# Prompt values in products of 512 columns instead of 256, norm weights spread by TensorE, the first stage's order on three engines written out

## The chip, the cores and the metric

One NeuronCore of one Trainium2 chip runs the whole program. Its engines work side by side, each through its own instructions in order: TensorE (PE, with PEld for its weight loads), VectorE (DVE), ScalarE (ACT), GpSimd (POOL) and SyncE (SP), which issues almost all DMAs of this kernel. The metric is the device time of one execution in microseconds (us); lower is better.

## What is computed

One layer of a hybrid encoder, for two groups with the same weights: a prompt of 1024 rows and a sample of 512 rows, 1024 columns each.

```python
def _rmsnorm(x, g):
    xf = x.astype(jnp.float32)
    y = xf * lax.rsqrt(jnp.mean(xf * xf, axis=-1, keepdims=True) + EPS)
    return (y * g.astype(jnp.float32)).astype(x.dtype)

def _layer(x, norm_g, w_in, ...):
    h = _rmsnorm(x, norm_g)
    proj = jnp.einsum('bld,de->ble', h, w_in)
    (q, f_fw, f_bw, i, z_a, c_B, c_C, c_x, z_b, g_a, g_b) = jnp.split(proj, SPLIT_POINTS, axis=-1)
    o_a = _hgrn2_bidir(q, i, f_fw, f_bw, lb_fw, lb_bw, hnorm_g)
    ...
    return x + jnp.einsum('bld,de->ble', merged, w_o)
```

The change touches only the first stage: the norm h of both groups, and the prompt's part `i` of the projection (the values, 1024 rows by 1024 columns, contraction over 1024).

## The kernel before

A number in float32 is split into a high part (a rounded copy, made by ACT) and a low part (the rest, a subtraction on DVE); `split` at L61 to L64 does that. A product of two split operands is three matmuls (`PASSES`: high by high, high by low, low by high), summed in PSUM.

The first stage works on twelve tiles of 128 rows: tiles 0 to 7 are the prompt, 8 to 11 the sample. For each tile: load (L86), sum of squares on ACT (L92), epsilon on DVE (L93), the power -0.5 on POOL (L81), two multiplications by that and by the norm weights on DVE (L96), eight transposes on PE (L163), and then, for a prompt tile, two splits into the operands `B11`, `B12`, `B21`, `B22` (tiles `s0`, `B12`, `s4`, `s6`), for a sample tile two copies and stores to `hs_d` (L230, L231).

Between the tiles stand the value products. The 1024 columns of weights are taken in four blocks of 256. `value_weights` (L184) loads a block in four pieces of 256 KB, each of two rows of 128, into two buffers `v_raw`, and splits them into buffers `v_h` and `v_l`, seven of each, so that three of the next block's four pieces can be made while the present block is in use. `prompt_values` (L196) makes for each prompt tile 24 matmuls of 256 columns (8 contraction steps by 3 passes, L201), one copy from PSUM to SBUF on ACT (L204) and a store to `v_d` on SP (L205). During the last two blocks DVE and ACT also make the sums `T1` to `T4` of the operands for the next stage (`mixed`, L174), which borrow the two large buffers `w2_raw` of the next stage.

The next stage, `project2` (L281), begins with two loads of 512 KB into `w2_raw` (L286): the first has the blocks a11 and a12, the second a21 and a22. a11 is split for the first product (12 matmuls of 512 columns, L308); four sums on DVE (L290 to L293) are needed before the second. Its pools are opened before the last two blocks of values.

The norm weights are loaded by one DMA that repeats them on all 128 partitions (`gain`, 512 KB, L210). Fourteen matmuls on a tile of zeros (L215) run while nothing is there yet.

In what order the engines and SP's queue take these instructions is set by a scheduler that goes by the program's order and its own estimates; each queue is fixed when the program is built. An instruction at the head of a queue that waits for a semaphore holds all behind it on that queue. Each DMA also uses one of eight semaphores in turn.

## Time and profile before

| | us |
|---|---|
| median of 3 runs (lowest to highest) | 1933.41 (1932.57 to 1936.35) |
| the profiled execution | 1938.16 |
| its span, first to last instruction | 1936.4 |
| PE busy in the span | 1911.7 (99%) |
| DVE busy | 1457.9 (75%) |
| ACT busy | 941.7 (49%) |
| POOL busy | 152.8 (8%) |
| mean granted clock of TensorE, share of full speed | 0.995 |

The profile shows one execution. Busy is the time in which an engine has an instruction under way. The granted clock is 1.0 at 2.4 GHz and 0.5 at 1.2 GHz. "Landing" of a DMA is the time from its issue to the arrival of its last byte. The first value product starts at 11.53 us, the first product of the next stage at 118.56 us, both from the span's start.

### The profile page before, as it was taken

What the parts mean: (1) busy time and instruction counts of PE and PEld (TensorE: products, weight loads), DVE (VectorE), ACT (ScalarE), POOL (GpSimd) and SP (SyncE); (2) the same over time, 40 slices, a digit from 0 to 9 for tenths busy, and PEclk for the clock granted to TensorE, in tenths of its full rate; (3) what the DMA queues carried; (4) which work ended last, traced back from release to release, by engine and by line L of the source; (5) the groups of instructions that cost most, each with busy time, mean ns of one, the idle gap of its engine ahead of it and who ended that gap; (6) DMA issues with size and microseconds to landing.
All of it is one profiled execution on the core that took longest, in us unless ns stands there. A gap on an engine that the chain in (4) does not pass through costs nothing.

```text
span 1936.4 us, 38016 instructions
## 1 busy us (share of the span) xinstructions
PE 1911.7 (99%) x14772; PEld 1612.7 (83%) x14772; DVE 1457.9 (75%) x2423; ACT 941.7 (49%) x1946; POOL 152.8 (8%) x220
## 2 busy tenths in 40 slices
PE   8999999999999999999999999999999999999898
PEld 8988888888888888887888888888888888888786
DVE  7558787878787878786677578777872558898896
ACT  6433434434343444444587567777683333424432
POOL 1000000000000000002122122222220000000000
PEclk8999999999999999999999999999999999999999
DMA  7466666766667676668855555655544966979852
GB/s 214 125 211 231 234 230 234 236 232 231 235 228 238 224 234 237 222 217 319 283 186 196 213 198 181 220 192 187 194 167 168 331 219 196 298 239 308 274 169 76
DMA packets 306436, 427.35 MB, mean 221 GB/s; under 512 B 26192, under 2 KB 178000, under 8 KB 306256
## 3 DMA queue, kind: packets, MB, share of 16 engines
q1 hardware_dynamic: 306256, 424.93, 65.0%
q8 instruction: 116, 1.90, 0.4%
q14 instruction: 64, 0.52, 0.1%
HBM read 254.98 MB, written 169.87 MB: 219 GB/s over the span
## 4 chain that ended last, share of the span: by engine, by line
PE 87%; DMA 5%; DVE 5%; issue 1%; ACT 1%; SPq 0%; POOL 0%; DVEq 0%; POOLq 0%; ACTq 0%
PE pp L308 39%; PE pp L77 21%; PE pw L825 9%; PE pp L201 5%; PE o L537 3%; PE sc L451 3%; PE u L513 2%; PE pp L70 2%; DMA w_raw<-in_w_a 1%; PE u L500 1%; DVE w_l L64 1%; DVE s_l L64 1%; PE sc L485 1%; DMA io<-oz_p 1%; DMA w_l<-wv_d 1%
## 5 line engine op out<-in xcount | busy, mean ns | idle before, releaser
L308 PE MATMUL pp<-s_h,w_h 128*128 128x512 f32 x1120 | 435.9, 389 | 1.2 <-ACT w_h L63 1.2
L308 PE MATMUL pp<-s_l,w_h 128*128 128x512 f32 x1120 | 435.7, 389 | 0.0
L308 PE MATMUL pp<-s_h,w_l 128*128 128x512 f32 x1120 | 435.7, 389 | 0.0
L63 ACT ACTIVATE w_h<-w_raw 128x512 fp32r<-128x512 f32 (+1 forms) x204 | 141.3, 693 | 230.7 <-PE pp L308 151.7
L77 PE MATMUL pp<-s_h,w_h 128*128 128x512 f32 x632 | 250.6, 397 | 2.0 <-ACT K L132 2.0
L308 PEld LDWEIGHTS pp<-s_h,w_h 128*128 128x128 f32 x1120 | 210.2, 188 | 45.4 <-ACT w_h L63 1.9
L308 PEld LDWEIGHTS pp<-s_l,w_h 128*128 128x128 f32 x1120 | 210.2, 188 | 43.6
L308 PEld LDWEIGHTS pp<-s_h,w_l 128*128 128x128 f32 x1120 | 210.2, 188 | 43.6
L77 PE MATMUL pp<-s_h,w_l 128*128 128x512 f32 x632 | 246.4, 390 | 0.0
L77 PE MATMUL pp<-s_l,w_h 128*128 128x512 f32 x632 | 246.2, 390 | 0.0
L313 DVE TENSOR_TENSOR tmp<-pp,tmp 128x512 f32<-128x512 f32 x240 | 165.5, 690 | 106.2 <-PE pp L308 105.0
L63 ACT ACTIVATE w_h<-w_S 128x512 fp32r<-128x512 f32 x160 | 99.4, 628 | 187.9 <-PE pp L308 80.9
L64 DVE TENSOR_TENSOR w_l<-w_raw,w_h 128x512 fp32r<-128x512 f32 (+1 forms) x204 | 155.8, 765 | 37.6 <-ACT w_h L63 37.1
L825 PE MATMUL pw<-s_h,w_h 128*128 128x512 f32 x392 | 153.4, 391 | 2.6 <-ACT w_h L63 2.6
L825 PE MATMUL pw<-s_h,w_l 128*128 128x512 f32 x392 | 153.3, 391 | 2.6 <-DVE w_l L64 2.6
L825 PE MATMUL pw<-s_l,w_h 128*128 128x512 f32 x392 | 153.2, 391 | 0.0
L435 ACT COPY cat<-K 128x512 f32<-128x512 f32 x168 | 111.6, 667 | 65.5 <-DVE K L437 26.9
L77 PEld LDWEIGHTS pp<-s_h,w_h 128*128 128x128 f32 x632 | 118.8, 188 | 25.5 <-ACT K L132 2.4
L77 PEld LDWEIGHTS pp<-s_h,w_l 128*128 128x128 f32 x632 | 118.6, 188 | 25.3
L77 PEld LDWEIGHTS pp<-s_l,w_h 128*128 128x128 f32 x632 | 118.9, 188 | 23.4
L436 ACT COPY cat<-Q 128x512 f32<-128x512 f32 x168 | 112.0, 667 | 29.2 <-DVE Q L438 22.3
L437 DVE TENSOR_TENSOR K<-K,T 128x512 f32<-128x512 f32 x144 | 108.9, 756 | 22.9 <-ACT cat L435 21.0
(187 smaller groups left out, 3301.5 us busy)
## 6 DMA issues: line engine op xcount, KB each, us to landing
w_raw<-in_w_in SPq DMA_DIRECT2D x80, 512.0 KB, 5.3
ws_d<-w_h SPq DMA_DIRECT2D x160, 256.0 KB, 2.5
ws_d<-w_l SPq DMA_DIRECT2D x160, 256.0 KB, 2.5
w_h<-ws_d SPq DMA_DIRECT2D x79, 512.0 KB, 3.7
w_l<-ws_d SPq DMA_DIRECT2D x79, 512.0 KB, 5.3
fkq_d<-sg SPq DMA_DIRECT2D x48, 256.0 KB, 2.3
v_raw<-in_w_in SPq DMA_DIRECT2D x32, 256.0 KB, 3.4
fkq_d<-sk SPq DMA_DIRECT2D x32, 256.0 KB, 2.3
```

Source lines behind the costliest of these rows:

```text
L63: A.activation(hi, src, AF.Copy)
L64: V.tensor_tensor(lo, src, hi.bitcast(F32), op=ALU.subtract)
L77: T.matmul(out, whl[a][:, k, :], rhs(k, b), start=k == 0 and n == 0, stop=k == KT - 1 and n == 2)
L201: T.matmul(pp, B[f"B{k // 4 + 1}{t + 1}"][a][:, k % 4, c * P:(c + 1) * P], parts[k][b], start=k == 0 and m == 0, stop=k == KT - 1 and m == 2)
L308: T.matmul(bank, hl[x][:, k, :], B[b][y][:, k, :], start=k == 0 and i == 0, stop=k == 3 and i == 2)
L313: V.tensor_tensor(out, p, t, op=ALU.add)
L435: A.copy(ap(cat, 0, [[2 * hs, nb], [hs, 2], [1, hs]]), kall)
L436: A.copy(ap(cat, TB, [[2 * hs, nb], [hs, 2], [1, hs]]), qall)
L437: V.tensor_tensor(kall, kall, ap(t, m + 1, [[2, nb], [-m - 1, 2], [0, hs]]), op=ALU.mult)
L451: T.matmul(k.sc[-1][s * Q32:(s + 1) * Q32, li % 4, c, :], kk[:, o:o + Q32], qq[:, t:t + Q32], start=True, stop=True)
L537: T.matmul(p[:, c, :], l, r, start=m == 0, stop=m == len(mms) - 1)
L825: T.matmul(bank, hl[x][:, c:c + P], O[n][y][:, k, :], start=k == 0 and i == 0, stop=k == 3 and i == 2)
```

## The change

- The value weights are taken in two blocks of 512 columns instead of four of 256: 24 matmuls of 512 columns for each tile and block, 384 in all instead of 768, with 16 copies and stores instead of 32, each twice as large. A piece of weights is one row of 128 by 512 columns (256 KB as before), so there are eight pieces in a block.
- The first block's eight pieces are loaded at the very start into the two large buffers `mix` and split by `first_parts`; for three of them the subtraction is on POOL. The second block's go through `value_parts`, two buffers `v_raw`, and `v_h`, `v_l` with nine buffers each.
- `gain` comes from two loads of one partition (2 KB each, issued by ACT, as is that of the identity) and two matmuls of a row of ones by them, copied from PSUM by DVE. There are 6 and 2 warming matmuls in place of 14.
- The order of PE, ACT and DVE in the first stage is written out: tile i + 1 is transposed in the middle of the products of tile i, eight transposes in one piece. What comes after (`mixed`, the last five tiles' products) is written out for PE alone. SP's order is still the scheduler's.
- The pools `rp`, `cs`, `wp` of the next stage are opened after the last value product, not before the last two blocks.

```diff
-WARM = 14
+WARM, WARM_2 = 6, 2
 
...
-        vst, p0st = ExitStack(), ExitStack()
+        vst, p0st, mxst = (ExitStack() for _ in range(3))
         wv, pv = (vst.enter_context(tc.tile_pool(name=n, bufs=1)) for n in ("wv", "pv"))
         psv = vst.enter_context(tc.tile_pool(name="psv", bufs=1, space=PSUM))
+        mx = mxst.enter_context(tc.tile_pool(name="mx", bufs=2, side="right"))
         p0 = p0st.enter_context(tc.tile_pool(name="p0", bufs=2, side="right"))
         B["B12"] = [pv.tile([P, 4, TB], F32R, name=f"B12_{s}") for s in "hl"]
 
...
+        xt, rn = {}, {}
+        def x_load(i):
+            xt[i] = p0.tile([P, D], F32, name="x_sb", bufs=4)
+            load(xt[i], x_tiles[i])
+        def square(i):
+            ss = p0.tile([P, 1], F32, name="ss", bufs=3)
+            A.activation(p0.tile([P, D], F32, name="junk", bufs=1), xt[i], AF.Square, scale=D ** -0.5, accum_out=ss)
+            V.tensor_scalar_add(ss, ss, EPS)
+            rn[i] = rsqrt(p0, ss, "x")
+        def scaled(i):
+            y = xt[i]
+            for c in range(0, D, 512):
+                V.scalar_tensor_tensor(y[:, c:c + 512], y[:, c:c + 512], rn[i], gain[:, c:c + 512],
+                                       op0=ALU.mult, op1=ALU.mult)
+        def transposed(i):
+            for half in range(2):
+                tp = psv.tile([P, 4, P], F32, name="tp", bufs=4)
+                for k in range(4):
+                    T.transpose(tp[:, k, :], xt[i][:, (4 * half + k) * P:(4 * half + k + 1) * P], ident)
+                yield half, tp
+        def tile_parts(i, half, tp):
+            cols = slice(i % CPB * P, (i % CPB + 1) * P)
+            if i < 8:
+                split(*(z[:, :, cols] for z in B[f"B{half + 1}{i // CPB + 1}"]), tp)
+            else:
+                t = p0.tile([P, 4, P], F32, name="hs")
+                A.copy(t, tp)
+                store(hs_d[:, 4 * half:4 * half + 4, cols], t)
 
         def mixed(k):
-            t = wp.tile([P, 4, TB], F32, name="w2_raw", bufs=2)
+            t = mx.tile([P, 4, TB], F32, name="mix")
...
 
...
+        parts = {}
+        def value_rows(col, k):
+            c0 = SPLIT["i"] * P + col
+            return w["w_in"][k * P:(k + 1) * P, c0:c0 + TB]
+        def value_tiles(k):
+            parts[k] = [wv.tile([P, TB], F32R, name=f"v_{s}", bufs=9) for s in "hl"]
+            return parts[k]
+        def value_parts(col, k):
+            raw = wv.tile([P, TB], F32, name="v_raw", bufs=2)
+            load(raw, value_rows(col, k))
+            split(*value_tiles(k), raw)
+        def products(i, pp, ks):
+            for k in ks:
+                for m, (a, b) in enumerate(PASSES):
+                    T.matmul(pp, B[f"B{k // 4 + 1}{i // CPB + 1}"][a][:, k % 4, i % CPB * P:(i % CPB + 1) * P], parts[k][b],
+                             start=k == 0 and m == 0, stop=k == KT - 1 and m == 2)
+        def bank_v():
+            return psv.tile([P, TB], F32, name="pp", bufs=4)
+        def values_out(i, col, pp):
+            s = mx.tile([P, TB], F32, name="st")
+            A.copy(s, pp)
+            store(v_d[i, :, col:col + TB], s)
+        order = ExitStack()
+        order.enter_context(tc.manual_schedule(engines={T.engine, A.engine, V.engine}))
+        x_load(0)
+        gain_row = [mx.tile([P, TB], F32, name="st")[0:1, :] for _ in range(2)]
+        for c, g in enumerate(gain_row):
+            nc.scalar.dma_start(g, w["norm_g"][:, c * TB:(c + 1) * TB])
+        nc.scalar.dma_start(ident, ident_d)
+        raws = [mx.tile([P, 4, TB], F32, name="mix") for _ in range(2)]
+        for k in range(KT):
+            load(raws[k // 4][:, k % 4, :], value_rows(0, k))
+            if k == 1:
+                x_load(1)
+        x_load(2)
+        x_load(3)
+        idle = p0.tile([P, P], F32, name="idle", bufs=1)
+        V.memset(idle, 1.0)
         gain = p0.tile([P, D], F32, name="gain", bufs=1)
-        x_ahead = [x_tile(p0, 0)]
-        load(ident, ident_d)
-        load(gain, w["norm_g"].to_broadcast([P, D]))
-        idle = p0.tile([P, P], F32, name="idle", bufs=1)
-        V.memset(idle, 0.0)
-        for n in range(WARM):
-            T.matmul(psv.tile([P, 4, P], F32, name="tp", bufs=4)[:, 0, :], idle, idle, start=True, stop=True)
-        pure(0)
-        parts = value_weights(0)
-        pure(1)
-        prompt_values(0, parts, 0)
-        for c in range(2, CPB):
-            pure(c)
-            prompt_values(0, parts, c - 1)
-        prompt_values(0, parts, CPB - 1)
-        parts = value_weights(256)
-        for c in range(CPB):
-            y = normed(p0, 8 + c, gain)
-            for half in range(2):
-                t = p0.tile([P, 4, P], F32, name="hs")
-                A.copy(t, transposed(y, half))
-                store(hs_d[:, 4 * half:4 * half + 4, c * P:(c + 1) * P], t)
-            prompt_values(256, parts, c)
+        def warm(n):
+            for _ in range(n):
+                T.matmul(psv.tile([P, 4, P], F32, name="tp", bufs=4)[:, 0, :], idle, idle, start=True, stop=True)
+        warm(WARM)
+        for c, row in enumerate(gain_row):
+            g = psv.tile([P, 4, P], F32, name="tp", bufs=4).rearrange("p a b -> p (a b)")
+            T.matmul(g, idle[0:1, :], row, start=True, stop=True)
+            V.tensor_copy(gain[:, c * TB:(c + 1) * TB], g)
+        warm(WARM_2)
+        def first_parts(k):
+            raw, (hi, lo) = raws[k // 4][:, k % 4, :], value_tiles(k)
+            A.activation(hi, raw, AF.Copy)
+            (G if k in (2, 4, 6) else V).tensor_tensor(lo, raw, hi.bitcast(F32), op=ALU.subtract)
+        square(0)
+        scaled(0)
+        tps = list(transposed(0))
+        first_parts(0)
+        tile_parts(0, *tps[0])
+        first_parts(1)
+        tile_parts(0, *tps[1])
+        first_parts(2)
+        square(1)
+        first_parts(3)
+        scaled(1)
+        first_parts(4)
+        first_parts(5)
+        pp = bank_v()
+        products(0, pp, range(6))
+        tps = list(transposed(1))
+        first_parts(6)
+        first_parts(7)
+        for x in tps:
+            tile_parts(1, *x)
+        square(2)
+        scaled(2)
+        products(0, pp, range(6, 8))
+        values_out(0, 0, pp)
+        def ahead_of(i):
+            if i + 3 < 12:
+                x_load(i + 3)
+            if i + 2 < 12:
+                square(i + 2)
+            yield
+            if i + 1 < 12:
+                for x in list(transposed(i + 1)):
+                    tile_parts(i + 1, *x)
+            if i + 2 < 12:
+                scaled(i + 2)
+            yield
+        for i in range(1, 8):
+            todo = ahead_of(i)
+            next(todo)
+            pp = bank_v()
+            products(i, pp, range(4))
+            next(todo)
+            if i == 7:
+                for k in range(4):
+                    value_parts(TB, k)
+            old = dict(parts)
+            products(i, pp, range(4, 8))
+            values_out(i, 0, pp)
+        for k in range(4, KT):
+            value_parts(TB, k)
+        for i in range(8, 11):
+            todo = ahead_of(i)
+            next(todo)
+            pp = bank_v()
+            products(i - 4, pp, range(4))
+            next(todo)
+            products(i - 4, pp, range(4, 8))
+            values_out(i - 4, TB, pp)
+        order.close()
+        order.enter_context(tc.manual_schedule(engines={T.engine}))
 
...
-        parts = value_weights(512)
         p0st.close()
+        for n, i in enumerate((7, 0, 1, 2, 3)):
+            if n < 4:
+                mixed(n)
+            pp = bank_v()
+            products(i, pp, range(KT))
+            values_out(i, TB, pp)
+        order.close()
+        mxst.close()
+        vst.close()
         rp = outer.enter_context(tc.tile_pool(name="rp", bufs=1, side="right", reuse_waits="tile"))
         cs = right.enter_context(tc.tile_pool(name="cs", bufs=1, side="right", reuse_waits="tile"))
         wp = st.enter_context(tc.tile_pool(name="wpp", bufs=1, side="right", reuse_waits="tile"))
-        for col in (512, 768):
-            if col > 512:
-                parts = value_weights(col)
-            for c in range(CPB):
-                prompt_values(col, parts, c)
-                if c % 2 == 0:
-                    mixed((col - 512) // 128 + c // 2)
-        vst.close()
```

From the first dozen instructions of the next stage on, the order on every engine is the same in both programs. Three places where it differs follow. A number in a name is that of one tile.

SP's queue around the change from one block of weights to the next, before (`v_raw_977` to `v_raw_995` are the four pieces of the third block, `st_586` is the last tile of the first):

```order
L205 DMA v_d_67<-st_502 128x256
L191 DMA v_raw_609<-in_w_in 128x2x256
L191 DMA v_raw_977<-in_w_in 128x2x256
L205 DMA v_d_67<-st_530 128x256
L205 DMA v_d_67<-st_558 128x256
L191 DMA v_raw_983<-in_w_in 128x2x256
L191 DMA v_raw_989<-in_w_in 128x2x256
L205 DMA v_d_67<-st_586 128x256
L231 DMA hs_d_66<-hs_623 128x4x128
L231 DMA hs_d_66<-hs_631 128x4x128
```

The same place now (`v_raw_644` to `v_raw_689` are pieces 2 to 7 of the second and last block, `st_590` and `st_668` are the outputs of tiles 6 and 7 from the first):

```order
L219 DMA v_d_67<-st_590 128x512
L179 DMA hs_d_66<-hs_624 128x4x128
L179 DMA hs_d_66<-hs_627 128x4x128
L204 DMA v_raw_644<-in_w_in 128x512
L204 DMA v_raw_650<-in_w_in 128x512
L219 DMA v_d_67<-st_668 128x512
L204 DMA v_raw_671<-in_w_in 128x512
L204 DMA v_raw_677<-in_w_in 128x512
L204 DMA v_raw_683<-in_w_in 128x512
L204 DMA v_raw_689<-in_w_in 128x512
```

Before, pieces of a later block stand among the stores of an earlier one; now six of the second block's eight stand around and behind the last store of the first block. `v_raw_644` waits for the subtraction of piece 0 and `v_raw_650` for that of piece 1, and so on by twos.

ACT at the same place now (`v_h_634` to `v_h_652` are the high parts of pieces 0 to 3, `pp_601` is the bank of tile 7):

```order
L178 COPY hs_624<-tp_614 128x512
L178 COPY hs_627<-tp_619 128x512
L63 ACTIVATE v_h_634<-v_raw_632 128x512
L63 ACTIVATE v_h_640<-v_raw_638 128x512
L63 ACTIVATE s2_h_92<-mix_883 128x512
L63 ACTIVATE s1_h_90<-mix_883 128x512
L63 ACTIVATE s5_h_98<-mix_883 128x512
L63 ACTIVATE v_h_646<-v_raw_644 128x512
L63 ACTIVATE v_h_652<-v_raw_650 128x512
L218 COPY st_668<-pp_601 128x512
```

and before:

```order
L204 COPY st_558<-pp_533 128x256
L63 ACTIVATE v_h_607<-v_raw_609 128x512
L63 ACTIVATE v_h_975<-v_raw_977 128x512
L204 COPY st_586<-pp_561 128x256
L230 COPY hs_623<-tp_624 128x512
L230 COPY hs_631<-tp_632 128x512
```

Pieces 2 and 3 of the new block now stand ahead of the copy of tile 7's output, which stood behind one piece of a block two further on.

SP's queue at the end of the stage, before (`st_1236` to `st_1389` have six more outputs behind them; `w2_raw_1558` is the first pair of the next stage):

```order
L205 DMA v_d_67<-st_1236 128x256
L286 DMA w2_raw_1558<-in_w_in 128x8x128
L205 DMA v_d_67<-st_1264 128x256
L286 DMA w2_raw_1558<-in_w_in 128x8x128
L205 DMA v_d_67<-st_1316 128x256
L300 DMA ws_d_69<-w2_h_1570 128x512
L205 DMA v_d_67<-st_1344 128x256
```

and now (`st_1088` is the output of the last value product, `w2_raw_1111` the first pair of the next stage):

```order
L219 DMA v_d_67<-st_970 128x512
L219 DMA v_d_67<-st_1015 128x512
L219 DMA v_d_67<-st_1060 128x512
L448 DMA v_raw_1785<-in_w_in 128x512
L219 DMA v_d_67<-st_1088 128x512
L373 DMA w2_raw_1111<-in_w_in 128x8x128 x2
L373 DMA w2_raw_1276<-in_w_in 128x8x128
```

Both loads that the next stage begins with have moved from among the stores to behind the last of them.

## Rows read from the trace of the kernel before

**Rows 1.** The chain that ended last, by engine (page, part 4).

```profile
PE 87%; DMA 5%; DVE 5%; issue 1%; ACT 1%; SPq 0%; POOL 0%; DVEq 0%; POOLq 0%; ACTq 0%
```

**Rows 2.** Stretches: length; busy us (instructions) by engine; granted clock, DMA share, GB/s.

```profile
15.00:19.00 4.00, 3.65 (x17) 3.65 (x18) 2.75 (x7) 3.31 (x7) 1.07 (x2) 0.50 0.76 259
60.00:100.00 40.00, 40.00 (x337) 40.00 (x336) 28.72 (x49) 17.95 (x36) 0.00 (x0) 1.00 0.36 105
118.50:123.00 4.50, 3.30 (x15) 2.42 (x15) 2.49 (x6) 1.87 (x4) 0.00 (x0) 1.00 0.30 87
```

**Rows 3.** PE in order of time: first and last value product from 100 us on.

```profile
100.08 0.28 PE L201 MATMUL pp<-v_h,s_l 128*128 128x256 f32 x1
...
118.44 0.28 PE L201 MATMUL pp<-v_h,s_l 128*128 128x256 f32 x1
```

**Rows 4.** PE in order of time: 512-column products of the next stage, first and last.

```profile
328.91 0.39 PE L308 MATMUL pp<-s_h,w_h 128*128 128x512 f32 x1
...
344.78 0.39 PE L308 MATMUL pp<-s_l,w_h 128*128 128x512 f32 x1
```

**Rows 5.** PE in order of time: transposes among value products (start, us, idle before).

```profile
26.32 0.28 PE L201 MATMUL pp<-v_h,s_l 128*128 128x256 f32 x1
26.44 0.60 PE L163 MATMUL tp<-ident,x_sb 128*128 128x128 f32 x4
26.79 0.36 PE L201 MATMUL pp<-v_h,s_h 128*128 128x256 f32 x1
26.99 0.28 PE L201 MATMUL pp<-v_l,s_h 128*128 128x256 f32 x1
...
33.06 0.63 PE L163 MATMUL tp<-ident,x_sb 128*128 128x128 f32 x4 [0.66 <-issue]
```

**Rows 6.** The start in order of time, PE and DVE.

```profile
1.08 5.51 PE L215 MATMUL tp<-idle 128*128 128x128 f32 x28 [1.08 <-DVE idle L213]
7.80 1.41 DVE L96 SCALAR_TENSOR_TENSOR x_sb<-x_sb,rs_x,gain 128x512 f32<-128x512 f32 x2 [1.90 <-DMA gain<-in_norm_g]
11.53 0.58 PE L201 MATMUL pp<-v_h,s_h 128*128 128x256 f32 x1 [1.09 <-ACT s_h L63]
```

**Rows 7.** Groups by line and shape: xcount, busy us, mean ns, idle before; POOL's over the span.

```profile
L92 ACT ACTIVATE junk<-x_sb 128x1024 f32<-128x1024 f32 x12 | 12.7, 1057 | 11.1 <-DMA x_sb<-in_x_prompt 6.6 <-POOL rs_x L81 3.7 <-DMA x_sb<-in_x_sample 0.9
L63 ACT ACTIVATE v_h<-v_raw 128x512 fp32r<-128x512 f32 x16 | 10.1, 629 | 4.6 <-DMA v_raw<-in_w_in 3.7 <-PE pp L201 0.6
L64 DVE TENSOR_TENSOR v_l<-v_raw,v_h 128x512 fp32r<-128x512 f32 x16 | 10.9, 688 | 21.0 <-ACT v_h L63 21.0
L425 POOL TENSOR_TENSOR T<-F 128x512 f32<-128x512 f32 x24 | 27.6, 1151 | 1006.4 <-DMA F<-fkq_d 849.2 <-DVE Q L438 93.7 <-DVE F L134 63.6
```

**Rows 8.** Landings by tile: `v_raw` (66 to 95 us), then `w2_raw` (90 to 112 us).

```profile
DMA to landing us min/median/max: 2.8/2.9/3.0
...
DMA to landing us min/median/max: 4.1/4.8/5.9
```

**Rows 9.** What SP's queue waited for, first 125 us: total us, times, longest.

```profile
SPq L205 <- ACT st L204: 45.3, 25, 2.8
SPq L191 <- DVE v_l L64: 14.1, 9, 3.5
```

**Rows 10.** The end of the values in order of time: ACT, SP, ACT, PE.

```profile
118.80 0.37 ACT L204 COPY st<-pp 128x256 f32<-128x256 f32 x1 [2.51 <-PE pp L201]
119.61 0.38 SPq L361 DMA_DIRECT2D v_raw<-in_w_in  x1
121.50 0.59 ACT L317 COPY tmp<-pp 128x512 f32<-128x512 f32 x1 [2.33 <-PE pp L308]
122.67 0.50 PE L308 MATMUL pp<-s_h,w_h 128*128 128x512 f32 x1 [1.20 <-ACT w_h L63]
```

**Rows 11.** Late in the program: PE in order of time, then the stretch's granted clock.

```profile
1812.91 0.50 PE L825 MATMUL pw<-s_h,w_h 128*128 128x512 f32 x1 [1.00 <-ACT w_h L63]
1815.26 0.63 PE L825 MATMUL pw<-s_h,w_l 128*128 128x512 f32 x1
1817.39 0.63 PE L825 MATMUL pw<-s_l,w_h 128*128 128x512 f32 x1
...
1815.00:1818.00 3.00, 3.00 (x9) 2.33 (x8) 3.00 (x5) 2.43 (x4) 0.00 (x0) 0.50 0.84 278
```

More of the change, by code (lines that the diff above doesn't have):

```diff
@@ L82, in rsqrt @@
         return r
-    def x_tile(pool, i):
-        y = pool.tile([P, D], F32, name="x_sb", bufs=5)
-        load(y, x_tiles[i])
-        return y
-    def normed(pool, i, gain, ahead=()):
-        y = ahead.pop(0) if ahead else x_tile(pool, i)
-        ss = pool.tile([P, 1], F32, name="ss")
-        A.activation(pool.tile([P, D], F32, name="junk", bufs=1), y, AF.Square, scale=D ** -0.5, accum_out=ss)
-        V.tensor_scalar_add(ss, ss, EPS)
-        r = rsqrt(pool, ss, "x")
-        for c in range(0, D, 512):
-            V.scalar_tensor_tensor(y[:, c:c + 512], y[:, c:c + 512], r, gain[:, c:c + 512], op0=ALU.mult, op1=ALU.mult)
-        return y
     keep = ctx.enter_context(tc.tile_pool(name="keep", bufs=1, reuse_waits="tile"))
@@ L157, in trunk_kernel @@
         B["B12"] = [pv.tile([P, 4, TB], F32R, name=f"B12_{s}") for s in "hl"]
-        def transposed(y, half):
-            tp = psv.tile([P, 4, P], F32, name="tp", bufs=4)
-            for k in range(4):
-                T.transpose(tp[:, k, :], y[:, (4 * half + k) * P:(4 * half + k + 1) * P], ident)
-            return tp
-        def pure(c):
-            for t in range(2):
-                y = normed(p0, t * CPB + c, gain, x_ahead)
-                for half in range(2):
-                    n, cols = f"B{half + 1}{t + 1}", slice(c * P, (c + 1) * P)
-                    tp = transposed(y, half)
-                    split(*(z[:, :, cols] for z in B[n]), tp)
+        xt, rn = {}, {}
@@ L182, in mixed @@
                 split(*(z[:, k, :] for z in B[n]), q[x])
-        def value_weights(col):
-            parts = []
-            for k in range(0, KT, 2):
-                hl = [wv.tile([P, 2, 256], F32R, name=f"v_{s}", bufs=7) for s in "hl"]
-                raw = wv.tile([P, 2, 256], F32, name="v_raw", bufs=2)
-                c0 = SPLIT["i"] * P + col
-                load(raw, w["w_in"][k * P:(k + 2) * P, c0:c0 + 256].rearrange("(k p) c -> p k c", p=P))
-                split(*hl, raw)
-                parts += [[z[:, i, :] for z in hl] for i in range(2)]
-            return parts
@@ L196, in prompt_values @@
-        def prompt_values(col, parts, c):
-            for t in range(2):
-                pp = psv.tile([P, 256], F32, name="pp", bufs=4)
-                for k in range(KT):
-                    for m, (a, b) in enumerate(PASSES):
-                        T.matmul(pp, B[f"B{k // 4 + 1}{t + 1}"][a][:, k % 4, c * P:(c + 1) * P], parts[k][b],
-                                 start=k == 0 and m == 0, stop=k == KT - 1 and m == 2)
-                s = pv.tile([P, 256], F32, name="st", bufs=2)
-                A.copy(s, pp)
-                store(v_d[t * CPB + c, :, col:col + 256], s)
```

1 line of the change is left out of this document (removed).

## The prediction

> **What bounds the kernel now.** First the chain of waits by engine: PE holds 87% of it, DMA and DVE 5% each [rows 1]. So time is won by shortening PE's own work or lost by leaving it idle, and an engine beside it counts only where PE waits for it. Then the same stretch of values by windows: from 60 to 100 us PE is busy 40.00 of 40.00 at clock 1.00, while DVE is at 28.72, ACT at 17.95 and the DMAs at 0.36 [rows 2]. Nothing waits there, although SP's queue waits 25 times for a copy on ACT (45.3 us in all) and nine times for a subtraction of weights (14.1 us) [rows 9]: these waits are covered by loads that stand a block ahead. The two ends are another matter. Between 15 and 19 us PE is busy 3.65 of 4.00 at clock 0.50, and from 118.5 to 123 it works 3.30 of 4.50 [rows 2]. Since the order of every engine is the same from the first dozen instructions of the next stage on, only the first 123 us can change. I count up to the start of the second product of the next stage, 122.67 us [rows 10], and add what changes to the profiled execution's 1938.16 us, which is 4.75 above the median of 1933.41.
>
> **Products, −5.1.** From the first to the last row there are 153 steps in 18.36 us, 0.1200 each [rows 3]; 512 columns take 70 steps in 15.87 us, 0.2267 each [rows 4]. 768 × 0.1200 = 92.2 becomes 384 × 0.2267 = 87.1. All of it lies on PE's path. In cycles at 2.4 GHz the rows are 288 and 544, each 32 over the columns.
>
> The Trainium skill ("TensorE: Matmul & The Clock Gate", section "Back-to-back issue gap") gives a warm gap of N/2.4 + 2.5 ns, which speaks against this change: two small products would cost only 2.5 ns more than one large one. By that the term would be 384 × 2.5 ns = 1.0 us, an estimate from the page, and the sum below +16.1 in place of +12.0. The rows show an excess of 13 ns a product, so here the measurement decides.
>
> **Transposes, −0.5.** A group of four makes the step from 26.44 to its last neighbour longer: 26.32 to 26.99 is 0.67 with two products of 0.12 in it, so 0.43 a group [rows 5]. There are 24 groups, 10.3 us. Twelve groups of eight lose one change of kind each; I take 0.78 a group, with 0.74 to 0.86 as bounds (−1.4 to 0; I use −1.0 to 0, as two buffers must be free at once). **Bubble, −0.7.** Idle 0.66 ahead of the transposes at 33.06, put down to PE's own issue [rows 5], belongs to a place in the old order that is gone; −0.8 to 0.
>
> **Start, −1.8.** Before, 118.56 us (118.44 + 0.12) less 92.2, 10.3 and the bubble of 0.8 leaves 15.3 us that PE lost at the start. The first scaling waits 1.90 us for the repeated load of `gain` and starts at 7.80; the first product starts at 11.53 [rows 6]. Now `gain` comes from 2 KB loads, two products of a row of ones, and two copies. No row has such a product. 512 columns in one pass at the low clock took 0.427 (2.13 / 5) [rows 11]; a warming product of 128 columns takes 5.51 / 14 = 0.39 [rows 6], and four times that is 1.6. So 0.43 to 1.6 each, and a copy like a subtraction, 0.69 [rows 7]. With the square (1.06 us [rows 7]) running beside it, scaling starts between 7.4 and 9.2, and the first product, which no longer has the second half's scaling and other tiles' work ahead of it, at 9.9 to 11.7; I take 10.8. From there 18 products at 0.427 end at 18.5, eight transposes at 19.1, six products at 0.227 at 20.5. By then 24 × 0.227 + 2 × 0.78 = 7.0 us of work is done, so 13.5 is lost. Bounds −3.0 to +1.0 (a POOL subtraction of 512 columns takes 1.15 us [rows 7] and three stand in this chain).
>
> **The second block's weights, +10.3.** Here the wide pieces are made through two `v_raw` buffers, and each raw buffer is free only when its subtraction on DVE is done. The order of SP shows pieces 2 to 7 around and behind the last store of the first block; each pair must go round: load issued, landing 2.9 [rows 8], split 0.63, subtraction 0.69 [rows 7], with 0.1 for the next issue 4.3 us, and 4.4 to 4.6 with the second of a pair. PE consumes a pair of rows in 6 × 0.227 = 1.36. In the old order the same waits existed [rows 9], but the pieces stood a block earlier and the spare buffers held three of four. Now seven spare pieces are missing: eight buffers of nine are still read by the last tile of the first block, which is followed at once by the second block.
>
> Let 0 be the start of tile 6's products (near 52 us). Tiles 6 and 7 are 2 × (5.44 + 0.78) = 12.4, so the second block could start at 12.4 and have its first tile done at 18.7. Piece 0 is ready about then: DVE has the scaling, `mixed` sums and the two subtractions in one queue. Piece 2 loads only then, and on ACT its split stands behind three `mixed` splits, each of which waits for a sum on DVE; seven DVE instructions of about 0.69 stand between the subtractions of piece 1 and piece 2, so that is 17.1, piece 3 at 17.8. The store of tile 7 waits for ACT's copy (0.59 [rows 10]) and holds piece 4 behind it on SP until 17.9; it lands at 20.9 and is ready at 22.4, piece 5 at 23.6, pieces 6 and 7 (loads at 22.5 and 23.7) at 26.9 and 28.2. PE's last three products end at 29.0. 29.0 − 18.7 = 10.3. Bound below 8 (landings of 2.8 and `mixed` work one step earlier), above 12.5 (another 0.7 on each of three round trips). What the store and copy wait for cost nothing before, since the cover was a whole block.
>
> **Clock, +2.5.** Late in the program, after PE had idled 1.00 us, the stretch 1815 to 1818 was at 0.50 with PE busy 3.00 of 3.00 [rows 11]; at the start the clock was still 0.50 at 15 to 19 us, up to 7.5 us after the first product [rows 2, 6]. A PE starved in pieces of 2 to 4 us should fall to the low level and be held there when it is fed again. A low stretch of 3.0 to 7.5 us loses about half; I take 5.2 us, 2.5. Bounds 0 to 3.4.
>
> **Next stage's weights, +7.3.** Before, both loads of `w2_raw` stood among the stores, six outputs ahead of the end, and the first product followed the last value product directly. Now both stand behind the last store, which waits for ACT's copy of the last product. With T as the end of values: copy 0.1 + 0.59, store issue 0.38 [rows 10], so loads go out at T + 1.1; landing 4.4, between the lowest 4.1 and the median 4.8 [rows 8] as little else is in flight; split 0.63; PE at T + 6.3. It has then idled longest of all, so twelve products at 0.427 take 5.1, and the second product starts at T + 11.4; its own operands (0.69 sum, 0.63, 0.69 behind the second load) are there by T + 9. Before this was 122.67 − 118.56 = 4.1. So +7.3; 5.9 with landing 4.1 and the clock rising half way, 8.5 with landing 5.6.
>
> **Sum.** −5.1 − 0.5 − 0.7 − 1.8 + 10.3 + 2.5 + 7.3 = +12.0: profiled 1950.2, median 1945.4. All ends low give +4.0 (1937.4), all high +20.3 (1953.7).
>
> **Rivals.** *Worse on ACT and DVE* (1950, chance 0.14): the written order puts copies for the sample's tiles and `mixed` splits ahead of weight splits, and one late sum holds all. Each of the three round trips grows by 0.9 and a second low stretch of 5 us follows: +2.7 and +2.4, sum +17. For it: DVE already has 28.72 of 40 us [rows 2].
>
> *PE stays fed* (faster; 1925.3, chance 0.06): the second block's pieces keep ahead as they did [rows 9] and the next loads find their cover, so only −5.1 − 0.5 − 0.7 − 1.8 = −8.1 remains. This needs both stalls away; it decides the sign where together they (with the clock) cost less than 8.1 us. Against it, a pair takes over 4.3 us round and PE uses it in 1.36, and the loads of the next stage stand literally behind the last store.
>
> *Only the end stalls* (same; 1932.6, chance 0.07): −8.1 + 7.3 = −0.8, if the early pieces land while tile 7 is still running. *Only the weights stall* (1938.1, slower, chance 0.04): −8.1 + 12.8 = +4.7, if PE's idle time at the end is covered by work of the first products as before.
>
> *Products gain little* (1949.5, chance 0.03): if 0.1200 holds waits that wide products inherit and both forms run at their columns alone, 5.1 becomes 1.0. The rows of both forms are back to back [rows 3, 4], which speaks against it; the page above is the rule behind this one.
>
> **How the numbers follow.** The forecast, both stalls, has 0.66. A time within 0.2% (3.9 us, about what a measurement here can tell) is 1929.5 to 1937.3. Slower: 0.66 + 0.14 + 0.04 + 0.03 = 0.87, less 0.02 for the forecast's lowest edge, 0.85; same 0.07 + 0.02 = 0.09; faster 0.06. The range 1936 to 1952 takes in the forecast's bounds but for its highest edge, and three rivals; it leaves out the two rivals that lack the weights' stall.
>
> **What would show it.** *Products:* starts 0.227 apart in the first block; 0.24 would be wrong. *Start:* first product at 10.8, tile 1's at 20.5, no wait of scaling for `gain`. *Weights:* PE idle in pieces of 2 to 4 us between about 65 and 81 us ahead of products on `v_h`, `v_l`, ended by ACT, DVE or the load of `v_raw`; no gap over 1 us there would fell the forecast. *Clock:* 0.50 in that stretch and some us behind it. *End:* last value product at about 123, the first of the next stage at 129.6 after 6 us idle, ended by the split of `w2_raw`, the second at 134.7. If the next stage's first product starts before 119 us, the prediction is wrong.

## The result, and the profile after

The changed kernel takes 1950.66 us (median of 5 runs, 1947.78 to 1952.05) where the kernel before takes 1934.07 (5 runs, 1932.57 to 1936.35). The ratio is 1.0077, with a 95% interval of 1.0066 to 1.0089: slower. In a second comparison beside other kernels the medians were 1947.59 and 1935.58, ratio 1.0068 (1.0052 to 1.0084). The forecast was 1945.4, slower by 12.0, range 1936 to 1952.

The traces say where it is lost. Before, the second product of the next stage starts at 122.67 us [rows 10]; now at 135.17. That is 12.5 us, all in the first stage. At the end of the program the two traces are 13.9 us apart (spans 1950.3 and 1936.4); the other 1.4 is told at after_again. The page's first row for PE is

```profile
PE 1916.6 (98%) x14380; PEld 1595.2 (82%) x14380; DVE 1460.3 (75%) x2422; ACT 937.9 (48%) x1930; POOL 158.0 (8%) x223
```

PE is busy 4.9 us longer than before, although it has fewer products to do: products at the low clock count as busy. So busy time hides the loss, and the rows in order of time show it. First the start, PE (start, us, engine, line, operation, what it waited for in brackets):

```profile
3.94 3.78 PE L247 MATMUL tp<-st,idle 1*128 1x512 f32 x4
...
11.79 0.79 PE L210 MATMUL pp<-v_h,s_h 128*128 128x512 f32 x1
...
15.37 0.63 PE L210 MATMUL pp<-v_h,s_l 128*128 128x512 f32 x1
15.80 0.50 PE L210 MATMUL pp<-v_h,s_h 128*128 128x512 f32 x1
16.13 0.39 PE L210 MATMUL pp<-v_l,s_h 128*128 128x512 f32 x1
...
19.63 0.50 PE L210 MATMUL pp<-v_l,s_h 128*128 128x512 f32 x1 [1.88 <-DVE v_l L255]
...
25.18 1.03 PE L169 MATMUL tp<-ident,x_sb 128*128 128x128 f32 x8
25.97 0.48 PE L210 MATMUL pp<-v_h,s_h 128*128 128x512 f32 x1
26.29 0.39 PE L210 MATMUL pp<-v_l,s_h 128*128 128x512 f32 x1
```

The two products for the norm weights take 3.78 us together. The first value product starts at 11.79, before at 11.53 [rows 6]. Steps of 0.43 us up to 15.80 are the low clock, 0.23 from 16.13 on the high one. The wait of 1.88 at 19.63 is for the low part of the first block's piece 5: its subtraction on DVE stands behind the two scalings of tile 1, which last 3.51 us (see e12p_no_pool). The last three rows price a group of eight transposes: from 25.18 to 26.29 is 1.11, less one product of 0.227, is 0.88.

Then the place where the second block of weights begins, PE:

```profile
70.57 0.76 PE L210 MATMUL pp<-v_h,B_h 128*128 128x512 f32 x1 [2.15 <-ACT v_h L63]
71.79 0.79 PE L210 MATMUL pp<-v_l,B_h 128*128 128x512 f32 x1 [0.46 <-DVE v_l L64]
...
80.04 0.50 PE L210 MATMUL pp<-v_h,s_h 128*128 128x512 f32 x1 [1.49 <-ACT v_h L63]
80.83 0.78 PE L210 MATMUL pp<-v_l,s_h 128*128 128x512 f32 x1 [0.29 <-DVE v_l L64]
...
82.69 0.63 PE L210 MATMUL pp<-v_h,s_l 128*128 128x512 f32 x1
```

The tile that starts with the second block (at 66.89) ends at 82.69 + 0.43 = 83.12: 16.2 us where 24 x 0.227 + 0.88 = 6.3 are needed. Only 4.4 of the missing 9.9 stand as idle time in brackets; the rest is products at the low clock and short gaps within them. What PE waits for, in the order of the queues (SP, then ACT, then DVE):

```profile
66.95 0.95 SPq L204 DMA_DIRECT2D v_raw<-in_w_in  x2
71.60 0.33 SPq L219 DMA_DIRECT2D v_d<-st  x1
72.03 6.08 SPq L204 DMA_DIRECT2D v_raw<-in_w_in  x4
...
69.37 0.63 ACT L63 ACTIVATE s_h<-mix 128x512 fp32r<-128x512 f32 x1 [0.57 <-DVE mix L187]
69.90 1.20 ACT L63 ACTIVATE v_h<-v_raw 128x512 fp32r<-128x512 f32 x2
...
66.24 1.29 DVE L64 TENSOR_TENSOR v_l<-v_raw,v_h 128x512 fp32r<-128x512 f32 x2
71.05 1.29 DVE L64 TENSOR_TENSOR v_l<-v_raw,v_h 128x512 fp32r<-128x512 f32 x2
81.28 0.69 DVE L64 TENSOR_TENSOR v_l<-v_raw,v_h 128x512 fp32r<-128x512 f32 x1
```

Pieces 2 and 3 are loaded (66.95) when pieces 0 and 1 are subtracted (66.24); pieces 4 to 7 follow the store of tile 7 (71.60). Their landing took 2.9 us as before [rows 8]. The stretches as windows (length; busy us and instructions of PE, PEld, DVE, ACT and POOL; granted clock, DMA share, GB/s):

```profile
70.00:80.00 10.00, 7.47 (x20) 4.87 (x20) 10.00 (x17) 5.77 (x10) 0.00 (x0) 0.66 0.44 130
80.00:90.00 10.00, 9.67 (x38) 7.66 (x39) 9.12 (x18) 7.13 (x13) 1.72 (x2) 0.83 0.41 121
```

Before, PE was busy 40.00 of 40.00 here at clock 1.00 [rows 2]. Last the end of the values; PE, then SP and ACT:

```profile
123.39 0.39 PE L210 MATMUL pp<-v_h,s_l 128*128 128x512 f32 x1
129.89 0.79 PE L395 MATMUL pp<-s_h,w_h 128*128 128x512 f32 x1 [6.11 <-ACT w_h L63]
135.17 0.54 PE L395 MATMUL pp<-s_h,w_h 128*128 128x512 f32 x1
...
124.47 0.32 SPq L219 DMA_DIRECT2D v_d<-st  x1
124.84 1.18 SPq L373 DMA_DIRECT2D w_raw<-in_w_in  x2
...
129.21 0.63 ACT L63 ACTIVATE w_h<-w_raw 128x512 fp32r<-128x512 f32 x1 [4.76 <-DMA w_raw<-in_w_in]
```

The load goes out behind the last store (124.47), its split begins 4.37 us later, and the first twelve products take 5.28 us at the low clock.

### The profile page after: what moved, and what is told of

Same layout as the page of the kernel before. It is cut to its first block, busy times and chain, and to the rows that moved or that the text cites. A ratio compares the mean times of both kernels' runs of the same rounds, so it can differ in the third digit from the quotient of the medians.

```text
span 1950.3 us, 37174 instructions
## 1 busy us (share of the span) xinstructions
PE 1916.6 (98%) x14380; PEld 1595.2 (82%) x14380; DVE 1460.3 (75%) x2422; ACT 937.9 (48%) x1930; POOL 158.0 (8%) x223
## 4 chain that ended last, share of the span: by engine, by line
PE 85%; DVE 6%; DMA 5%; issue 2%; ACT 1%; SPq 0%; POOL 0%; DVEq 0%; POOLq 0%; ACTq 0%
PE pp L395 39%; PE pp L77 21%; PE pw L912 8%; PE pp L210 4%; PE o L624 3%; PE sc L538 3%; PE u L600 2%; PE pp L70 2%; DMA w_raw<-in_w_a 2%; PE u L587 1%; DVE w_l L64 1%; DVE s_l L64 1%; PE sc L572 1%; DMA w_l<-wv_d 1%; PE u L638 1%
```

## The experiments

My theory: the wide products gain what their rows say, and two places where the loads lost their cover take more than that back. The rivals: DVE, not the loads, is the bound at the second block; the wide products gain less. Ratios are to the kernel before. The edits are shown in part; `...` marks what is left out.

**e1_weights_ahead: the second block's pieces early.**

```diff
-            raw = wv.tile([P, TB], F32, name="v_raw", bufs=2)
-            load(raw, value_rows(col, k))
-            split(*value_tiles(k), raw)
+            split(*value_tiles(k), raws[k // 4][:, k % 4, :])
...
+        for n in range(2):      # behind values_out(0, 0, pp)
+            raws[n] = mx.tile([P, 4, TB], F32, name="mix")
+            for k in range(4):
+                load(raws[n][:, k, :], value_rows(TB, 4 * n + k))
```

> The changed kernel with one edit: the second block's eight pieces of value weights are loaded early, into the two large buffers `mix` (free between the first block's splits and the `mixed` sums), not one by one through two `v_raw`; their splits stand where they stood, the `mixed` sums come after them. Theory of the prediction (each pair of pieces had to go round through two buffers behind the last store of the first block): PE's idle time of about 4.4 us and the low clock between 68 and 85 us go, together some 10.7 us in the trace, 0 to 1 us of it stays; about 1940 us, 1.003 of before; the second block's products start about 68 us and follow each other at 0.227. Rival, DVE is the bound there (10.00 of 10.00 busy from 70 to 80 us), loads or not: PE goes on waiting for `v_l`, gain under 3 us, 1948 or more. The gap of 6.1 us ahead of the next stage stays in either case.

1937.55 us, ratio 1.0020 (1.0011 to 1.0029). PE in the stretch of the stall, and the gap at the end:

```profile
70.00:80.00 10.00, 10.00 (x54) 8.44 (x53) 9.12 (x18) 6.37 (x13) 1.72 (x2) 1.00 0.31 92
...
120.11 0.80 PE L400 MATMUL pp<-s_h,w_h 128*128 128x512 f32 x1 [6.10 <-ACT w_h L63]
```

The stall is gone and the clock stays at 1.00; the last value product starts at 113.63 and not at 123.39, 9.8 us earlier (10.7 expected). Most of the difference is a wait that the changed kernel does not have: near 42 us PE loses 0.6 us on the low part of tile 4's operands. The gap of 6.1 us is untouched. DVE is still busy 9.12 of 10. But the edit changed two things at once, the loads and the place of the sums.

**e1m_sums_later: the sums behind the pieces, the loads as changed.** It leaves out the line that gives ACT and DVE back to the scheduler:

```diff
-        order.close()
-        order.enter_context(tc.manual_schedule(engines={T.engine}))
```

> The changed kernel with one edit: the written order of ACT and DVE goes on to the end of the values, which puts all `mixed` sums and splits behind the second block's eight pieces; the pieces still go by twos through two `v_raw`. It tells apart what e1_weights_ahead did at once. In the trace of the changed kernel piece 2 landed at 69.85 us and its split began at 69.90, just behind a `mixed` split that waits for DVE: both were late at the same time. If the round of load, split and subtraction (4.3 to 4.5 us a pair) is enough by itself, most of the stall stays: last piece's subtraction 2 us earlier than in the changed kernel (81.3 to 82.0 there), 2 to 3 us of 10.7 gained, about 1945 us. Rival, the `mixed` work in DVE's queue was the cause: 7 us or more gained, 1941 or less. The gap of 6 us ahead of the next stage stays.

1954.15 us, ratio 1.0099 (1.0084 to 1.0114), slower than the changed kernel. DVE on the last piece, then two windows, then PE:

```profile
80.03 0.69 DVE L64 TENSOR_TENSOR v_l<-v_raw,v_h 128x512 fp32r<-128x512 f32 x1 [1.14 <-ACT v_h L63]
...
70.00:80.00 10.00, 7.56 (x23) 3.76 (x23) 3.34 (x5) 3.63 (x7) 0.00 (x0) 0.83 0.44 131
110.00:120.00 10.00, 10.00 (x45) 8.26 (x45) 9.86 (x16) 4.52 (x9) 0.00 (x0) 1.00 0.08 28
...
135.12 0.80 PE L393 MATMUL pp<-s_h,w_h 128*128 128x512 f32 x1 [12.46 <-ACT w_h L63]
```

From 70 to 80 us DVE is busy 3.34 of 10 in place of 10.00, and PE still only 7.56 in place of 7.47. The last subtraction is 1.25 us earlier (2 expected), the last value product 1.1 (122.28). So the round of the loads makes the stall by itself, and DVE's load was no cause that matters. What I had not seen: the sums now end too late. DVE is full from 100 to 120 us, `w_h` stands behind the last `mixed` splits on ACT, and the gap ahead of the next stage is 12.46 us where I had 6. My 1945 us missed that.

**e2_next_loads_early: the next stage's loads ahead of the last stores.**

```diff
-            s = mx.tile([P, TB], F32, name="st")
+            s = p0.tile([P, TB], F32, name="st") if col == 0 or 3 < i < 7 else wv.tile([P, TB], F32, name="v_raw", bufs=2)
```

The two rows of the norm weights take their buffers from `p0` as well.

> The changed kernel with one edit: the buffers `st` for the outputs lie in the pool `p0` (for the last five tiles the free `v_raw` are used), so that the pool `mx` holds only the `mixed` sums and ends before the last outputs; SP's queue then has the two loads of `w2_raw` ahead of the last five stores. Theory of the prediction (the next stage's first load waits in SP's queue behind the last store): the 6.1 us gap ahead of the first product of the next stage goes, and its twelve products run at 0.227 and not 0.427; 7.4 us in all, about 1943 us, 1.004 to 1.005 of before; the stall near 70 us stays as it was. Rival, the split of `w2_raw` waits for ACT and DVE, which are behind with `mixed`: gap shrinks to 3 to 4 us only, 1947.

1942.88 us, ratio 1.0047 (1.0033 to 1.0061), 7.8 us below the changed kernel's first median (1950.66) and 4.7 below its second (1947.59). The trace says more exactly what the edit is worth; PE:

```profile
121.82 0.39 PE L210 MATMUL pp<-v_h,s_l 128*128 128x512 f32 x1
122.04 0.39 PE L395 MATMUL pp<-s_h,w_h 128*128 128x512 f32 x1
126.13 0.50 PE L395 MATMUL pp<-s_h,w_h 128*128 128x512 f32 x1 [1.21 <-ACT w_h L63]
```

The next stage follows without a gap, at the high clock, and its second product comes 4.1 us after the first, as before [rows 10]. From the last value product to that second product it is 4.31 us, in the changed kernel 11.78: 7.5 us gained, 7.4 expected. (This execution stood 1.7 us ahead from the start; see after_again.)

**e12_both: both edits.**

> Both edits, the second block's pieces early and the next stage's loads ahead of the last stores. Theory of the prediction: the stalls add up, so both gains do; 5.1 us of the products and what the start and the bubble give stay; 1928 to 1933 us, 0.997 to 0.9995 of before; second product of the next stage at about 117 us where before has 122.67. Rival, each gap hides the other (the `mixed` sums now come later on DVE, after the weights, and the next stage needs them): the second product of the next stage waits for T2 and about 3 us come back, 1934 to 1937.

1931.67 us, ratio 0.9981 (0.9972 to 0.9990): faster than before. The second product of the next stage starts at 118.07 (117 expected), with the same 1.21 us of waiting as before, so the later sums are in time here:

```profile
118.07 0.50 PE L400 MATMUL pp<-s_h,w_h 128*128 128x512 f32 x1 [1.21 <-ACT w_h L63]
```

17.1 us against the changed kernel's 135.17: the two stalls and their clock are all that made it slower than before.

**e12p_no_pool: the first block's three subtractions from POOL to DVE, on top of e12_both.**

```diff
-            (G if k in (2, 4, 6) else V).tensor_tensor(lo, raw, hi.bitcast(F32), op=ALU.subtract)
+            V.tensor_tensor(lo, raw, hi.bitcast(F32), op=ALU.subtract)
```

> As with both edits, and the three subtractions of the first block's pieces that stood on POOL are on DVE. In the changed kernel two scalings of tile 1 took 3.51 us on DVE, beside two subtractions of 3.01 us on POOL, where two scalings take 1.42 alone; PE then waited 1.88 us for the last of POOL's subtractions. If the two engines slow each other there, DVE does the scalings in 1.4 and three subtractions in 2.1, and PE's gap of 1.88 us shrinks by 1 or more: 1 to 2 us less than both edits alone. Rival, DVE's queue only gets longer by 2.1 us: the same time or 1 us more.

1928.93 us, ratio 0.9973 (0.9963 to 0.9982). DVE and POOL of e12_both:

```profile
15.46 3.51 DVE L161 SCALAR_TENSOR_TENSOR x_sb<-x_sb,rs_x,gain 128x512 f32<-128x512 f32 x2
...
15.41 3.01 POOL L259 TENSOR_TENSOR v_l<-mix,v_h 128x512 fp32r<-128x512 f32 x2 [0.26 <-ACT v_h L258]
```

DVE and PE of e12p_no_pool:

```profile
15.45 1.41 DVE L161 SCALAR_TENSOR_TENSOR x_sb<-x_sb,rs_x,gain 128x512 f32<-128x512 f32 x2
16.78 2.49 DVE L259 TENSOR_TENSOR v_l<-mix,v_h 128x512 fp32r<-128x512 f32 x4
...
17.52 0.50 PE L208 MATMUL pp<-v_l,s_h 128*128 128x512 f32 x1 [0.74 <-DVE v_l L259]
```

Two scalings alone take 1.41, beside two subtractions on POOL 3.51. DVE has three more subtractions to do and is still done earlier. PE's gap of 1.89 ahead of piece 5 is gone; one of 0.74 stands ahead of piece 4. (The expectation put the old gap down to POOL's last subtraction; by the trace it ends with DVE's subtraction of piece 5, behind the slowed scalings.) Tile 1's products start at 21.04 and not at 22.46, 1.4 us earlier. The last value product starts at 111.48 and not at 113.76, 2.3 us earlier; the other 0.9 is mostly the wait near 42 us told at e1, which e12_both has and this kernel has not. Why it is gone here was not tested.

**p_half: the products as two of 256 columns, on top of e12p_no_pool.**

```diff
-                    T.matmul(pp, B[...][a][...], parts[k][b], ...)
+                    for c in range(0, TB, 256):
+                        T.matmul(pp[:, c:c + 256], B[...][a][...], parts[k][b][:, c:c + 256], ...)
```

> The kernel of e12p_no_pool, in which PE is fed without a gap from 18 us to the end of the values, with each value product of 512 columns as two of 256 into the two halves of its bank; nothing else is changed. By the rows of before (0.1200 for 256 columns, 0.2267 for 512) PE's path gets 384 x 0.0133 = 5.1 us longer: the last value product starts 5 us later than in e12p_no_pool. Rival, by the page's gap of N/2.4 + 2.5 ns: 384 x 2.5 ns = 1.0 us longer.

1933.18 us, ratio 0.9990 (0.9981 to 0.9999). The second product of the next stage, here and in e12p_no_pool:

```profile
120.30 0.50 PE L401 MATMUL pp<-s_h,w_h 128*128 128x512 f32 x1 [1.21 <-ACT w_h L63]
```
```profile
115.79 0.50 PE L400 MATMUL pp<-s_h,w_h 128*128 128x512 f32 x1 [1.20 <-ACT w_h L63]
```

4.5 us later, where 5.1 were forecast by the rows and 1.0 by the rule of the Trainium skill ("TensorE: Matmul & The Clock Gate", section "Back-to-back issue gap") that the prediction names. From the product that starts at 94.11 to the one at 115.94 there are 182 steps of 256 columns, 0.1200 each, as in rows 3: the price was right. What is short of 5.1 lies elsewhere: the first 13 of the 384 products stand ahead of a wait for DVE that ends at 17.52 in both kernels, which leaves 371 × 0.0133 = 4.9, and each tile with transposes in it gets only 0.29 longer and not 0.32.

**p_bcast: the norm weights by one repeated load as before, on top of e12p_no_pool.**

```diff
-        for c, g in enumerate(gain_row):
-            nc.scalar.dma_start(g, w["norm_g"][:, c * TB:(c + 1) * TB])
+        load(gain, w["norm_g"].to_broadcast([P, D]))
...
-            T.matmul(g, idle[0:1, :], row, start=True, stop=True)
-            V.tensor_copy(gain[:, c * TB:(c + 1) * TB], g)
+        warm(8 + WARM_2)
```

> The kernel of e12p_no_pool with the norm weights as they were before the change: one load of 512 KB that repeats them on all partitions, behind the first tile's load on SP, no products of a row of ones and no copies of their results; ten warming products stand in a row. With the products the first scaling starts at 9.18, after two copies of 0.69 that wait for two products of 1.7 each at the low clock. With the load it starts when the load has landed: 7.8 as in before if only that counts, first value product about 10.4 and not 11.8, 1.4 us gained. Rival, the 512 KB push the value weights' pieces back by 1.3 us (the DMAs are full from 5 to 15 us) and PE waits for those: same end, or up to 1 us later.

1928.30 us, ratio 0.9962 (0.9947 to 0.9976). PE:

```profile
8.95 0.50 PE L208 MATMUL pp<-v_h,s_h 128*128 128x512 f32 x1
15.35 0.50 PE L208 MATMUL pp<-v_l,s_h 128*128 128x512 f32 x1 [0.95 <-DVE v_l L253]
...
113.67 0.50 PE L394 MATMUL pp<-s_h,w_h 128*128 128x512 f32 x1 [1.21 <-ACT w_h L63]
```

The first scaling starts at 6.79 (7.8 expected), the first value product at 8.95, and the second product of the next stage is 2.1 us earlier than in e12p_no_pool. The first piece does come later for it (ACT begins its split at 7.53, after 1.60 us of waiting for the load, and at 5.55 in e12p_no_pool), but PE's wait at 15.35 is still for DVE. So the norm weights by products of a row of ones cost some 2 us at this place in this execution of e12p_no_pool. Where the two products run faster, as in after_again, the first scaling starts at 7.44 and little of that is left. The medians of the two kernels are too near to show it.

**p_early: the epsilon ahead of the copies, on top of e12p_no_pool.**

```diff
         warm(WARM)
+        square(0)
         for c, row in enumerate(gain_row):
...
             V.tensor_copy(gain[:, c * TB:(c + 1) * TB], g)
+            V.scalar_tensor_tensor(...)  # this half of tile 0
...
-        square(0)
-        scaled(0)
```

> The kernel of e12p_no_pool with the same norm weights' products, but tile 0's square, epsilon and power ahead of the copies in DVE's queue, and each half of tile 0 scaled right behind its half of the weights. The epsilon (8.37 us) then no longer stands behind the second copy, which waits for PE until 7.76: power done by 6.7, second half scaled by about 9.2 where it was 10.5; first value product 1.3 us earlier, the end of the values as much. Rival, the next thing late is the first pieces' landing (1.0 of the DMAs busy until 15 us): the gap ahead of piece 5 to 7 grows by as much and nothing is gained.

1927.23 us, ratio 0.9959 (0.9944 to 0.9974). The first value product starts at 9.67 (2.1 us earlier, 1.3 expected), the second product of the next stage 1.56 us earlier:

```profile
3.94 1.98 PE L252 MATMUL tp<-st,idle 1*128 1x512 f32 x4
...
114.23 0.50 PE L401 MATMUL pp<-s_h,w_h 128*128 128x512 f32 x1 [1.21 <-ACT w_h L63]
```

Not all of it is the edit's. The two products for the norm weights took 1.98 us in this execution and 3.78 in that of e12p_no_pool (see after_again), so the second copy on DVE started at 7.31 and not at 7.76. Up to 0.45 us is due to that; some 1.7 of the 2.1 and 1.1 or more of the 1.56 are left for the new order on DVE: the epsilon ahead of the copies, and each half of tile 0 scaled behind its own copy. The edit does both at once, so which of them gives how much stays open.

**p_warm: PE kept busy ahead of the transposes, on top of e12p_no_pool** (`WARM_2 = 5`, not 2).

> The kernel of e12p_no_pool with five warming products in place of two behind the products for the norm weights, so that PE idles 0.2 and not 1.1 us ahead of the first transposes. There the first nine value products ran 0.427 apart (low clock to 15.4 us) and PE then waited 0.74 us for DVE's subtraction of a piece until 17.52. If the clock holds the start back, the products run at 0.227 from 11.8 us on and 1.8 us are gained. If DVE's chain of pieces does, PE only waits longer there: value products go on at 17.5 as before, gain under 0.3 us.

1926.49 us, ratio 0.9958 (0.9941 to 0.9974). PE:

```profile
12.29 0.39 PE L208 MATMUL pp<-v_l,s_h 128*128 128x512 f32 x1
17.54 0.50 PE L208 MATMUL pp<-v_l,s_h 128*128 128x512 f32 x1 [0.96 <-DVE v_l L259]
...
115.97 0.50 PE L400 MATMUL pp<-s_h,w_h 128*128 128x512 f32 x1 [1.21 <-ACT w_h L63]
```

The clock is high from the first products on, and nothing is gained in the stage: the product at 17.5 waits for DVE as long as it takes (115.97 against 115.79 at the end). So DVE's chain of pieces bounds the start and the clock doesn't. The median is 2.4 us lower all the same, within the overlap of the intervals; by the trace it has no reason in this stage.

**after_again: the changed kernel once more.**

> The changed kernel once more, beside the runs that follow. In its trace PE stood 12.5 us behind before at the second product of the next stage and 13.95 us at the end, with a wait of 4.11 us for `w_h` near 1823 us that is 1.57 in before and 0.70 to 1.08 in two of the other traces; the medians differ by 16.6. If that late wait goes with the changed kernel, it is over 3 us here again; if it is chance of one execution, it is anywhere from 0.5 to 4 and the median lies 12 to 17 us above before (1.006 to 1.009).

1947.59 us, ratio 1.0068 (1.0052 to 1.0084). The late wait in the first execution, and then the products for the norm weights (3.78 in the first execution, above) and the late wait in this one; PE:

```profile
1822.79 0.80 PE L912 MATMUL pw<-s_h,w_h 128*128 128x512 f32 x1 [4.11 <-ACT w_h L63]
```
```profile
3.94 2.04 PE L247 MATMUL tp<-st,idle 1*128 1x512 f32 x4
...
1816.86 0.50 PE L912 MATMUL pw<-s_h,w_h 128*128 128x512 f32 x1 [0.59 <-ACT w_h L63]
```

The late wait of 4.11 us is 0.59 here (1.57 before, at most 2.13 in the other traces), so it is chance of one execution and not the change. So is a second thing: the two products for the norm weights took 2.04 and not 3.78 us, and the two warming products behind them 0.71 and not 1.22; by these steps the clock had risen early. The first value product started at 10.05, tile 1's at 20.71 (22.46 in the first execution), and the second product of the next stage at 133.59 (135.17). Of the ten traces of kernels with these products three (this one, e2 and p_early) have the short form. Both together move single executions of one kernel by 2 to 5 us, which is why a difference of 2 us between medians here says little and the row in the trace says more.

## Why the prediction held, step by step

The direction, the two mechanisms and their places were right. The forecast of the median was 5.3 us low against the first comparison (+16.6 measured, +12.0 forecast) and right against the second (+12.0). In the two traces the sum came to +12.5 and +10.9 at the second product of the next stage.

- **Products, −5.1.** Shown: p_half costs 4.5 with 371 of the 384 products on PE's path, and 0.1200 and 0.227 a product are what the traces have. The Trainium skill ("TensorE: Matmul & The Clock Gate", section "Back-to-back issue gap") gives its N/2.4 + 2.5 ns, which the prediction used, as the gap of isolated products. By it the difference would be 1.0, an estimate from the page; p_half does not agree with that.
- **Transposes, −0.5.** Wrong in sign, by little: a group of eight costs 0.88, so twelve cost 10.6 where 24 of four cost 10.3. The step that failed is that a longer group loses a change of kind. The product behind a group is late by 0.09 once and not by 0.08 twice, but the eight transposes take 0.79 to that product (25.18 to 25.97), where two groups of four take 0.70 (0.35 each, 26.44 to 26.79 [rows 5]).
- **Bubble, −0.7.** It held: in the first trace no idle time stands in brackets on PE from the product at 19.96 to the second block's first gap at 68.
- **Start, −1.8.** In the first trace it came to about 0: tile 1's products start at 22.46, not 20.5 (7.2 us of work done by then, 15.3 lost, as before). In after_again they start at 20.71, which is 13.5 lost, as forecast; the shorter products for the norm weights make the difference. Three terms failed. These two products took 1.9 us each, above my upper bound of 1.6 (1.0 in after_again). The epsilon stands behind the second copy in DVE's queue; I let it run beside (p_early, which also scales by halves: 1.1 us or more). And two subtractions on POOL made two scalings on DVE last 3.51, which I had priced as independent (e12p_no_pool: 1.4 us). That after_again meets the figure in spite of the last two is luck. The bound of +1.0 held.
- **Second block's weights, +10.3, and clock, +2.5.** The tile took 9.9 us too long, and three products at the low clock behind it (83.12 to 84.36) add 0.6: 10.5 and not 12.8. PE's idle pieces were 2.15, 0.46, 1.49 and 0.29 us, shorter than the 2 to 4 forecast; slow products filled the rest. The pieces were timed closely. With the start of tile 6 at 54.19 the subtractions ended 12.7, 17.6, 22.4, 23.6, 26.6 and 27.8 us behind it for pieces 0, 2, 4, 5, 6 and 7 (12.4, 17.1, 22.4, 23.6, 26.9, 28.2 forecast). The clock was over-sized, because most of the low stretch lies inside the stall, where PE waits anyway; only the six products that wait for no later piece pay for it, some 1.2 us where 2.5 were forecast. That split is worked out from the rows and was not tested by itself. e1 shows the size, e1m that the loads' round is enough and DVE's sums are no cause.
- **Next stage's weights, +7.3.** 11.55 us from the end of values to the second product, 4.1 before: +7.4. First product at 129.89 (129.6 forecast), second at 135.17 (134.7). e2 gives 7.5 back.

In the first trace the terms as measured are −5.1, +0.3, −0.8, 0, +10.5 and +7.4, together +12.3 of the +12.5. The sum was nearly right although terms were off: start and transposes gave some 2.6 less than forecast, and stall and clock took 2.3 less. That these cancel is luck. The rival in which PE stays fed (1925.3) could be built: e12_both has 1931.7, e12p_no_pool 1928.9. In its trace e12p_no_pool is 6.9 us ahead of before at the second product of the next stage, where the rival had 8.1; the transposes (0.8) and 0.4 of the start are what is missing.

The medians of p_bcast, p_early and p_warm are each 0.4% below before; the intervals do not tell them from e12p_no_pool. All of them are the wide products with the loads' cover put back.

## What to carry to other kernels

A change that makes one engine's work shorter also moves the loads in their queue. Ahead of it, list for each load which instruction of the queue it stands behind, and what that one waits for; here the load behind the last store of the stage cost its whole landing and the clock of what followed. Where a step becomes wider with buffers of the same size, the cover shrinks, so count how many pieces can be ready when the block changes. Before an engine's idle time is filled with another's work, look at whether the two slow each other.

## What the runs showed of the hardware that I had not expected

DVE and POOL slowed each other when both read two operands from SBUF: two scalings 3.51 and not 1.41 us, two subtractions on POOL 3.01, where one took 1.15 in the mean of another stage [rows 7]. From the first start to the last end it was 3.56 us, near the sum of 2 × 1.15 and 1.41. The Trainium skill ("SBUF — State Buffer", section "SBUF: two separate sides") states an exclusive lock between a DVE operation with two SBUF inputs and a GpSimd operation that reads SBUF; the rows agree with that.

A product of one row by 512 float32 columns took 1.9 us at the low clock and 1.0 where, by the steps behind it, the clock had risen, four and more times the 0.427 and 0.227 of the value products of 512 columns. In the first trace of the changed kernel the column of the granted clock read 1.00 from 10 to 15 us while products started 0.427 apart; there the steps tell the clock, not the column.
